# A two-block network on one core: exponentials' clamp and scaling on ScalarE, a later step, and VectorE in program order

## The chip, the cores and the metric

The kernel runs on one core of a Trainium2 chip. The metric is the device time of one execution in microseconds; for the kernel before it is the median of three runs. The engines are TensorE (PE; its weight loads are PEld), VectorE (DVE), ScalarE (ACT), GpSimd (POOL) and SyncE (SP), which issues most of the transfers.

## The reference, cut to what matters

A sequence of 256 tokens of width 1024 goes through a first block of two layers and a second block of two layers. In a layer of the first block, one wide projection feeds a state-space mixer (SSD) and a dilated attention; both are gated, merged, projected, and followed by a gated FFN. In a layer of the second block, one projection feeds a retention and a block-sparse attention; then come an output projection and a gate. The parts that the change touches:

```
# SSD, 32 heads in 4 groups, chunks of 128 tokens
a_cum = cumsum(dt * a)                         # per head, within a chunk
decay = exp(where(causal, a_cum[l] - a_cum[s], -inf))
y_diag = (c @ b.T * decay) @ (x * dt)
decay_states = exp(a_cum[-1] - a_cum)          # first chunk's state for the second
y = group_norm(y * silu(z)) * norm_w           # 4 groups

# dilated attention, 8 heads, three patterns per head
probs_g = exp(scores_g - lse_g);  out = sum_g softmax_g(lse)[g] * probs_g @ v

# entry of the second block
h = rms_norm(x) * norm_final;  u = rms_norm(h) * norm_g
v, q, k = u @ w_in ...
```

## The kernel before, in words

Every weight matrix is read in units of 128 x 1024 values, 488 in all. A unit comes by a transfer (two to a transfer), ScalarE casts it to its high half `wh` (L156), and the rest `wl` is a subtraction (L159), on VectorE, or on GpSimd for every fourth unit while `pool_every` is set, which is from after the dt path to the end of the SSD groups. TensorE then runs each product three times: high by high, high by low, low by high. There are three buffers for halves, and the next unit's halves are made two units ahead (`LEAD = 2`).

The side work (attention, SSD groups, group norms, norms) is written as generators. After each unit of matmuls `tick()` takes one step of each queue in `bg`; `drain` runs queues to their end. The order in which each engine gets its instructions is then set by a scheduler from the program's order and its own model of time, but for regions that `ordered(True, engines)` opens: there the named engines keep the order of the program. Before, only the start of the first block is such a region, and only for SyncE.

Attention (L498) takes four heads of a half, six steps a head: scores with mask and row maximum on VectorE, exponentials with row sums on ScalarE, two sums over the three patterns on GpSimd (L525, L526), a scaling by the reciprocal of the row sum on VectorE (L527, L528), and after two more steps the transposes on TensorE (L387). The first half's attention runs beside the projections of the second half, the second half's beside the B, C and SSD projections; it is drained in the third group at the latest.

An SSD group (L619) fetches the cumulated sums of its 8 heads, copied to all partitions, as `abc` by a transfer on GpSimd's queue (L623). For two heads a step, VectorE takes the minimum of `abc` and the row's own sum (L644), so that the exponent is never above 0; ScalarE makes six exponentials of 128 columns (L653), with the negated sum `nacum` or `rem` as bias; GpSimd multiplies by the masked products `cb` (L654). Two steps later TensorE uses the result (L664). `ssd_tail` (L677) is the group norm: squares, sums, a matmul, a power, a broadcast by matmul, four products (L699) and a split. A group is 12 units long: 4 of x, 4 of z, and 4 of the gate (groups 0 and 1) or of the attention branch (groups 2 and 3).

At the entry of the second block (`block2` with `l == 0`), `proj2` projects v and then q from the normed input before its row factor is known; meanwhile `n1.steps()` finds the factor (L234 to L244), makes the scaled u in four steps of two rows of tiles (L264, L380, L391), and at last scales h (L275).

Of the kernel before, what the change touches and what calls it, by code (L numbers as in the profile page):

```python
# [13 lines left out]
AF = mybir.ActivationFunctionType  # L14
ALU = mybir.AluOpType
# [3 lines left out]
P = 128  # L19
# [265 lines left out]
class Net:  # L285
# [209 lines left out]
            out.append(dst)  # L495
        return out

    def attention(self, v, kT, q0, q1, q2, oh, ol):  # L498
        nc = self.nc
        qs = (q0, q1, q2)  # L500
        scale = HD ** -0.5
        po = None
        for h in range(4):
            e = self.sp.tile([P, 3, 384], F32, tag="EM", name="E", bufs=3)
            m6 = self.small(8, "m6")
            for g in range(3):
                ps = self.ch.tile([P, 384], F32, tag="ch", name="ch")
                nc.tensor.matmul(ps[:, 0:256], qs[g][:, h, 128:256], kT[:, h, :], start=True, stop=True)
                nc.tensor.matmul(ps[:, 256:384], qs[g][:, h, 0:128], kT[:, h, 0:128], start=True, stop=True)
                nc.vector.tensor_tensor_reduce(e[:, g, 0:256], ps[:, 0:256], self.mask_a[:, g, 0:256], 1.0,  # L510
                                               -3e38, ALU.add, ALU.max, m6[:, g:g + 1])
                nc.vector.tensor_tensor_reduce(e[:, g, 256:384], ps[:, 256:384], self.mask_a[:, g, 256:384],
                                               1.0, -3e38, ALU.add, ALU.max, m6[:, 4 + g:5 + g])
            yield
            mx = self.small(4, "mx")
            nc.vector.tensor_reduce(mx[:, 0:2], m6.rearrange("p (i g) -> p i g", i=2)[:, :, 0:3],
                                    mybir.AxisListType.X, ALU.max)
            nc.vector.tensor_scalar(mx[:, 0:2], mx[:, 0:2], -scale, None, op0=ALU.mult)
            nc.scalar.activation(e[:, :, 0:256], e[:, :, 0:256], AF.Exp, bias=mx[:, 0:1], scale=scale,
                                 accum_out=mx[:, 2:3])  # L520
            nc.scalar.activation(e[:, :, 256:384], e[:, :, 256:384], AF.Exp, bias=mx[:, 1:2], scale=scale,
                                 accum_out=mx[:, 3:4])
            yield
            nc.vector.reciprocal(mx[:, 2:4], mx[:, 2:4])
            nc.gpsimd.tensor_tensor(e[:, 0, :], e[:, 0, :], e[:, 1, :], ALU.add)  # L525
            nc.gpsimd.tensor_tensor(e[:, 0, :], e[:, 0, :], e[:, 2, :], ALU.add)  # L526
            nc.vector.tensor_scalar(e[:, 0, 0:256], e[:, 0, 0:256], mx[:, 2:3], None, op0=ALU.mult)  # L527
            nc.vector.tensor_scalar(e[:, 0, 256:384], e[:, 0, 256:384], mx[:, 3:4], None, op0=ALU.mult)  # L528
            yield
            yield  # L530
            pt = self.transpose4([e[:, 0, 256:384], e[:, 0, 0:128], e[:, 0, 128:256]])
            pT = self.sp.tile([P, 384], F32, tag="pT", name="pT", bufs=2)
            nc.scalar.copy(pT, pt[:, 0:384])
            yield
            if h % 2 == 0:
                po = self.ch.tile([P, 2, S], F32, tag="ch", name="ch")
            vs = slice(128 * h, 128 * h + 128)
            nc.tensor.matmul(po[:, h % 2, :], v[:, 0, vs], pT[:, 0:256], start=True, stop=False)
            nc.tensor.matmul(po[:, h % 2, 128:256], v[:, 1, vs], pT[:, 256:384], start=False, stop=True)
            if h % 2:  # L540
                self.split(oh[:, h - 1:h + 1, :], ol[:, h - 1:h + 1, :], po)
            yield

    def dt_path(self, l, xh, xl, wd):

        nc = self.nc
# [13 lines left out]
        def tile2(tag):  # L560
            return self.sp.tile([P, 2, 32], F32, tag=tag, name=tag)

        x, e, z, z2, q = (tile2(n) for n in ("d_x", "d_e", "d_z", "d_z2", "d_q"))
        bias = self.rows[:, 2 * l:2 * l + 1, :].to_broadcast([P, 2, 32])
# [19 lines left out]
        dth = tile2("d_dth")  # L584
# [4 lines left out]
        nc.tensor.matmul(pc[:, 64:96], self.ones, adt[:, 0, :], start=True, stop=True)  # L589
        acum = tile2("d_acum")  # L590
        nc.vector.tensor_copy(acum, pc[:, 0:64].rearrange("p (c h) -> p c h", c=2))
        nacum = tile2("d_nacum")
        nc.vector.tensor_scalar(nacum, acum, -1.0, None, op0=ALU.mult)
        rem = self.small(32, "d_rem", 1)
        nc.vector.tensor_tensor(rem, pc[:, 64:96], acum[:, 0, :], ALU.subtract)
        pr = self.ch.tile([32, S], F32, tag="ch", name="ch")
# [3 lines left out]
        nc.scalar.copy(rows, pr)  # L600
        scr = self.dr.tile([32, S], F32, tag="scr", name="scr")
        nc.gpsimd.dma_start(scr, rows)
        return dth, acum, nacum, rem, scr

    def conv_pair(self, l, ps, ch, dst):

# [11 lines left out]

    def ssd_group(self, l, g, bc, xs, sz, dts, out, tails):  # L619
        nc = self.nc  # L620
        dth, acum, nacum, rem, scr = dts
        abc = self.sp.tile([P, 8, S], F32, tag="abc", name="abc")
        nc.gpsimd.dma_start(abc, scr[8 * g:8 * g + 8, :].partition_broadcast(P))  # L623
        pc = self.ch.tile([P, 384], F32, tag="ch", name="ch")
# [13 lines left out]
        for step in range(6):  # L638
            if step < 4:
                m = ms[step] = self.sp.tile([P, 2, 384], F32, tag="EM", name="M", bufs=3)  # L640
                h0 = 8 * g + 2 * step

                mb = m.rearrange("p j (b c) -> p j b c", b=3)
                nc.vector.tensor_tensor(  # L644
                    mb[:, :, 0:3:2, :], abc[:, 2 * step:2 * step + 2, :].rearrange("p j (b c) -> p j b c", b=2),
                    acum[:, :, h0:h0 + 2].rearrange("p b j -> p j b")[:, :, :, None].to_broadcast([P, 2, 2, P]),
                    ALU.min)
                for j in range(2):
                    hh = h0 + j
                    for b, src, bias in ((0, m[:, j, 0:128], nacum[:, 0, hh:hh + 1]),  # L650
                                         (1, abc[:, 2 * step + j, 128:256], rem[:, hh:hh + 1]),
                                         (2, m[:, j, 256:384], nacum[:, 1, hh:hh + 1])):
                        nc.scalar.activation(m[:, j, 128 * b:128 * b + 128], src, AF.Exp, bias=bias)  # L653
                nc.gpsimd.tensor_tensor(m, m, cb[:, None, :].to_broadcast([P, 2, 384]), ALU.mult)  # L654
            if step >= 2:
                pr = step - 2
                m = ms.pop(pr)
                if pr % 2 == 0:
                    yps = self.ch.tile([P, 2, S], F32, tag="ch", name="ch")

                for c, qs, ks in ((0, slice(0, 256), slice(0, 256)), (1, slice(128, 256), slice(256, 384))):
                    for j in range(2):
                        h = 2 * pr + j
                        nc.tensor.matmul(yps[64 * j:64 * j + 64, pr % 2, qs], xdt[:, c, 64 * h:64 * h + 64],  # L664
                                         m[:, j, ks], start=c == 0, stop=c == 1)
                if pr % 2:
                    for j in range(2):
                        f = pr - 1 + j
                        nc.vector.scalar_tensor_tensor(xs[:, f, :], xs[:, f, :], dsk[:, 4 * g + f:4 * g + f + 1],
                                                       yps[:, j, :], ALU.mult, ALU.add)  # L670
                    nc.gpsimd.tensor_tensor(xs[:, pr - 1:pr + 1, :], xs[:, pr - 1:pr + 1, :],
                                            sz[:, pr - 1:pr + 1, :], ALU.mult)
            if step == 5:
                tails.append(self.ssd_tail(l, g, xs, out))
            yield

    def ssd_tail(self, l, g, xs, out):  # L677
        nc = self.nc
# [1 line left out]
        nc.scalar.activation(sq, xs, AF.Square)  # L680
        nc.gpsimd.tensor_tensor(sq[:, 0:2, :], sq[:, 0:2, :], sq[:, 2:4, :], ALU.add)
        nc.gpsimd.tensor_tensor(sq[:, 0, :], sq[:, 0, :], sq[:, 1, :], ALU.add)
        for _ in range(4 if g == 3 else 6):
            yield
        pss = self.ch.tile([P, 2], F32, tag="ch", name="ch")
        for t in range(2):
# [16 lines left out]
    def block1(self, l, h, n1):  # L703
        nc = self.nc
        a = self.a
        qn, qa, qs, qt = [n1.steps()], [], [], []
# [19 lines left out]
        os = [self.pair([P, 4, S], "O0", "O1")]  # L726
# [9 lines left out]
        for f in range(0, 8, 2):  # L736
            ps = self.pairA("w_in", l, C_B + 128 * f, D, getu)
            self.conv_pair(l, ps, 16 + f, bc[:, f:f + 2, :])
            if f == 0:
                self.drain(qa)  # L740
                os.append(self.pair([P, 4, S], "A0", "A1"))
                qa.append(self.attention(*B, *os[1]))
        def halves(tiles):
            return [tiles[f // 4][:, f % 4:f % 4 + 2, :] for f in range(0, 8, 2)]

# [317 lines left out]
    def block2(self, l, x, n1):  # L1063
# [7 lines left out]
        def tile(tag, shape, bufs=1):  # L1071
            return sp.tile([P, *shape], F32, tag=tag, name="b2", bufs=bufs)

        qn, qm, qr = [n1.steps()], [], []
        self.bg = [qn, qm, qr]
        mv = tile("B2", [2, 512])
        self.proj2(l, 6, n1.get, "v", mv, norm=n1)
        if l == 0:
# [1 line left out]
        mq = tile("B0", [4, S])  # L1080
        self.proj2(l, 4, n1.get, "q", mq, qm, hg[:, 0, :], norm=n1)
        self.drain(qn)
        getu = n1.getv
        mk = tile("B1", [4, S])
        self.proj2(l, 5, getu, "k", mk, qm, hg[:, 1, :])
# [166 lines left out]
```

## Time and profile before

| | |
|---|---|
| median of 3 runs | 1570.98 us (1570.22 to 1572.79) |
| profiled execution | 1576.56 us, span 1574.8 us |
| PE busy | 1541.3 us |
| DVE busy | 1163.3 us |
| ACT busy | 826.6 us |
| POOL busy | 462.5 us |
| mean granted clock of TensorE | 0.993 |

The span is from the first instruction to the last. A busy time is the share of the span in which the engine had an instruction running; an engine that is idle and not on the path costs nothing. The granted clock is the share of TensorE's full clock; 1.00 is the full level and 0.50 the lower one.

### The profile page before, as it was taken

The numbers are of one execution on the slowest core, as the hardware profiler recorded it, in microseconds if no ns is written. First come the engines' busy times: TensorE is split into PE (matmuls) and PEld (weight loads), VectorE is DVE, ScalarE is ACT, GpSimd is POOL, SyncE is SP. The second block draws the span as 40 slices with busy tenths as digits, with TensorE's granted clock in tenths as the row PEclk, the third lists the DMA queues.
The fourth block names the chain that finished last, engine by engine and source line by source line (L and its number), as shares of the span: only waits on it lengthen the run. The fifth ranks groups of instructions, "written<-read, shape, count | busy, mean of one in ns | idle before, by whom it ended". The sixth has DMA issues, their size and how long they took to land.

```text
span 1574.8 us, 29400 instructions
## 1 busy us (share of the span) xinstructions
PE 1541.3 (98%) x12104; PEld 1478.2 (94%) x12104; DVE 1163.3 (74%) x1758; ACT 826.6 (52%) x1276; POOL 462.5 (29%) x285
## 2 busy tenths in 40 slices
PE   9999999989999999999999999999999999999998
PEld 7999999889999999999998999998999979998998
DVE  7888998765577565668897887567655578788776
ACT  6444567545455444544466765445444454456443
POOL 4656356543000000066525565110000112111110
PEclk9999999989999999999999999999999999999999
DMA  8644544445554555554443455455555545455542
GB/s 307 234 167 139 184 162 161 149 146 191 188 182 166 188 187 188 191 210 161 157 166 135 182 193 199 169 203 207 181 184 182 184 159 185 136 188 187 188 147 95
DMA packets 42662, 280.68 MB, mean 178 GB/s; under 512 B 4864, under 2 KB 7040, under 8 KB 10016
## 3 DMA queue, kind: packets, MB, share of 16 engines
q1 hardware_dynamic: 40592, 267.20, 47.9%
q0 software_dynamic: 1936, 11.60, 1.9%
q8 instruction: 95, 1.56, 0.4%
q14 instruction: 39, 0.32, 0.1%
HBM read 274.53 MB, written 4.26 MB: 177 GB/s over the span
## 4 chain that ended last, share of the span: by engine, by line
PE 85%; DVE 8%; ACT 2%; issue 2%; POOL 2%; DMA 1%; DVEq 0%; SPq 0%; POOLq 0%; ACTq 0%
PE mm L451 17%; PE mm L453 17%; PE mm L452 17%; PE mm L435 6%; PE mm L436 6%; PE mm L437 6%; PE mm L399 3%; PE mm L398 3%; PE mm L400 3%; DVE wl L159 2%; PE ch L664 1%; PE tr L387 1%; ACT wh L156 1%; DVE acc L614 1%; DVE E L527 1%
## 5 line engine op out<-in xcount | busy, mean ns | idle before, releaser
L156 ACT CAST wh<-raw 128x1024 fp32r<-128x1024 f32 x488 | 511.0, 1048 | 570.3 <-PE mm L452 381.6
L159 DVE TENSOR_TENSOR wl<-raw,wh 128x1024 fp32r<-128x1024 f32 x456 | 606.1, 1332 | 259.2 <-ACT wh L156 255.7
L453 PE MATMUL mm<-uh,wl 128*128 128x256 f32 x2240 | 629.3, 281 | 5.8 <-DVE wl L159 3.7
L451 PE MATMUL mm<-uh,wh 128*128 128x256 f32 x2240 | 633.2, 283 | 0.1
L452 PE MATMUL mm<-ul,wh 128*128 128x256 f32 x2240 | 627.5, 280 | 0.0
L453 PEld LDWEIGHTS mm<-uh,wl 128*128 128x128 f32 x2240 | 422.9, 189 | 7.3 <-DVE wl L159 4.6
L451 PEld LDWEIGHTS mm<-uh,wh 128*128 128x128 f32 x2240 | 422.6, 189 | 5.1 <-issue 3.5
L452 PEld LDWEIGHTS mm<-ul,wh 128*128 128x128 f32 x2240 | 425.0, 190 | 0.7 <-issue 0.3
L208 POOL TENSOR_TENSOR nsq<-nsq 128x512 f32<-128x512 f32 x19 | 29.7, 1570 | 484.6 <-ACT nsq L202 405.7
L159 POOL TENSOR_TENSOR wl<-raw,wh 128x1024 fp32r<-128x1024 f32 x32 | 79.0, 2470 | 68.2 <-ACT wh L156 63.1
L435 PE MATMUL mm<-A,wh 128*128 128x256 f32 x288 | 82.1, 285 | 1.0 <-ACT wh L156 1.0
L437 PE MATMUL mm<-A,wl 128*128 128x256 f32 x288 | 81.6, 285 | 0.1
L399 PE MATMUL mm<-wl,nu 128*128 128x512 f32 x192 | 77.1, 403 | 2.9 <-DVE wl L159 2.8
L654 POOL TENSOR_TENSOR M<-M,cb 128x768 f32<-128x768 f32 x32 | 69.8, 2197 | 25.7 <-ACT M L653 17.7
L400 PE MATMUL mm<-wh,nu 128*128 128x512 f32 x192 | 76.0, 399 | 0.0
L398 PE MATMUL mm<-wh,nu 128*128 128x512 f32 x192 | 72.6, 401 | 3.0 <-DVE tg L827 2.2
L614 DVE SCALAR_TENSOR_TENSOR acc<-mm,feat,acc 128x255 f32<-128x255 f32 (+1 forms) x144 | 67.2, 475 | 5.1 <-ACT acc L612 3.7
L471 POOL TENSOR_TENSOR qT<-qT,rot 64x512 f32<-64x512 f32 x32 | 56.7, 1773 | 48.5 <-ACT qT L467 48.5
L472 POOL TENSOR_TENSOR qT<-qT,rp 64x512 f32<-64x512 f32 x32 | 60.1, 1877 | 28.3 <-DVE rp L469 28.1
L436 PE MATMUL mm<-A,wh 128*128 128x256 f32 x224 | 63.8, 285 | 0.0
L435 PEld LDWEIGHTS mm<-A,wh 128*128 128x128 f32 x288 | 55.0, 191 | 1.4 <-ACT wh L156 1.3
L437 PEld LDWEIGHTS mm<-A,wl 128*128 128x128 f32 x288 | 54.8, 191 | 0.6 <-DVE wl L159 0.6
(311 smaller groups left out, 2984.3 us busy)
## 6 DMA issues: line engine op xcount, KB each, us to landing
raw<-in_w_dram SPq DMA_DIRECT2D x243, 1024.0 KB, 4.8
abc<-scr POOLq DMA_DIRECT2D x8, 1024.0 KB, 5.3
es<-e POOLq DMA_DIRECT2D x4, 512.0 KB, 4.3
e<-es SPq DMA_DIRECT2D x4, 512.0 KB, 4.5
raw<-in_w_dram SPq DMA_DIRECT2D x2, 512.0 KB, 4.4
h<-in_xT_dram SPq DMA_DIRECT2D x2, 512.0 KB, 9.4
h<-in_xT_dram SPq DMA_DIRECT2D x1, 1024.0 KB, 4.9
hs<-h POOLq DMA_DIRECT2D x1, 1024.0 KB, 5.9
```

What stands on the lines that cost most here:

```text
L156: self.nc.scalar.copy(h, raw)
L159: eng.tensor_tensor(lo, raw, h.bitcast(F32), ALU.subtract)
L398: nc.tensor.matmul(ps, xh[:, k0 + k, ts], hw[:, k, :], start=start and k == 0, stop=False)
L399: nc.tensor.matmul(ps, xh[:, k0 + k, ts], lw[:, k, :], start=False, stop=False)
L400: nc.tensor.matmul(ps, xl[:, k0 + k, ts], hw[:, k, :], start=False, stop=stop and k == 1)
L435: nc.tensor.matmul(ps, hw[:, n % 8, :], xh[:, kx, :], start=opens, stop=False)
L436: nc.tensor.matmul(ps, hw[:, n % 8, :], xl[:, kx, :], start=False, stop=False)
L437: nc.tensor.matmul(ps, lw[:, n % 8, :], xh[:, kx, :], start=False, stop=left[f] == 0)
L451: nc.tensor.matmul(ps, hw[:, k, :], xh[:, kx, :], start=j == 0 and k == 0, stop=False)
L452: nc.tensor.matmul(ps, hw[:, k, :], xl[:, kx, :], start=False, stop=False)
L453: nc.tensor.matmul(ps, lw[:, k, :], xh[:, kx, :], start=False, stop=j == n - 1 and k == 7)
L614: nc.vector.scalar_tensor_tensor(acc[:, j, k:S], ps[:, j, 0:S - k], w[:, 3 - k:4 - k], acc[:, j, k:S], ALU.mult, ALU.add)
```

## The change

Five edits. The clamp of the SSD exponents moves from a VectorE minimum to ScalarE: four Relu of 128 columns (of the row's sum minus `abc`), and one exponential over all four results with scale -1; the two `rem` exponentials stay. `nacum` is no longer made. The scaling of E in attention moves from VectorE to ScalarE. The second half's attention takes one step more in each head before its transposes. The group norms of groups 0 to 2 take one step more before their matmul. And in `block2` of its first layer VectorE keeps program order from the v projection to the end of `n1`'s steps.

```
-    def attention(self, v, kT, q0, q1, q2, oh, ol):
+    def attention(self, v, kT, q0, q1, q2, oh, ol, late=0):
...
-            nc.vector.tensor_scalar(e[:, 0, 0:256], e[:, 0, 0:256], mx[:, 2:3], None, op0=ALU.mult)
-            nc.vector.tensor_scalar(e[:, 0, 256:384], e[:, 0, 256:384], mx[:, 3:4], None, op0=ALU.mult)
-            yield
-            yield
+            nc.scalar.activation(e[:, 0, 0:256], e[:, 0, 0:256], AF.Identity, scale=mx[:, 2:3])
+            nc.scalar.activation(e[:, 0, 256:384], e[:, 0, 256:384], AF.Identity, scale=mx[:, 3:4])
+            yield
+            yield
+            for _ in range(late):
+                yield
...
-        nacum = tile2("d_nacum")
-        nc.vector.tensor_scalar(nacum, acum, -1.0, None, op0=ALU.mult)
...
-                nc.vector.tensor_tensor(
-                    mb[:, :, 0:3:2, :], abc[:, 2 * step:2 * step + 2, :].rearrange("p j (b c) -> p j b c", b=2),
-                    acum[:, :, h0:h0 + 2].rearrange("p b j -> p j b")[:, :, :, None].to_broadcast([P, 2, 2, P]),
-                    ALU.min)
                 for j in range(2):
                     hh = h0 + j
-                    for b, src, bias in ((0, m[:, j, 0:128], nacum[:, 0, hh:hh + 1]),
-                                         (1, abc[:, 2 * step + j, 128:256], rem[:, hh:hh + 1]),
-                                         (2, m[:, j, 256:384], nacum[:, 1, hh:hh + 1])):
-                        nc.scalar.activation(m[:, j, 128 * b:128 * b + 128], src, AF.Exp, bias=bias)
+                    a2 = abc[:, 2 * step + j, :]
+                    for c in range(2):
+                        nc.scalar.activation(mb[:, j, 2 * c, :], a2[:, 128 * c:128 * c + 128], AF.Relu, scale=-1.0,
+                                             bias=acum[:, c, hh:hh + 1])
+                    nc.scalar.activation(mb[:, j, 1, :], a2[:, 128:256], AF.Exp, bias=rem[:, hh:hh + 1])
+                nc.scalar.activation(mb[:, :, 0:3:2, :], mb[:, :, 0:3:2, :], AF.Exp, scale=-1.0)
...
-        for _ in range(4 if g == 3 else 6):
+        for _ in range(4 if g == 3 else 7):
             yield
...
-                qa.append(self.attention(*B, *os[1]))
+                qa.append(self.attention(*B, *os[1], 1))
...
+        if l == 0:
+            self.ordered(True, {mybir.EngineType.DVE})
         mv = tile("B2", [2, 512])
         self.proj2(l, 6, n1.get, "v", mv, norm=n1)
...
         self.drain(qn)
+        self.ordered(False)
```

## Rows read from the trace of the kernel before

**Rows 1.** Page, part 1: busy us, share of the span, instructions.
```profile
PE 1541.3 (98%) x12104; PEld 1478.2 (94%) x12104; DVE 1163.3 (74%) x1758; ACT 826.6 (52%) x1276; POOL 462.5 (29%) x285
```

**Rows 2.** Waits of TensorE, 90 to 260: us in total, times, longest.
```profile
PE tr L387 <- DVE E L528: 2.4, 3, 1.2
PE mm L453 <- DVE wl L159: 1.1, 1, 1.1
```

**Rows 3.** Waits of TensorE, 270 to 360.
```profile
PE mm L453 <- DVE wl L159: 4.8, 2, 2.4
PE mm L453 <- POOL wl L159: 1.9, 1, 1.9
PE tr L387 <- DVE xs L617: 1.5, 2, 0.7
```

**Rows 4.** Waits of TensorE, 720 to 860.
```profile
PE mm L453 <- DVE wl L159: 2.5, 2, 1.3
PE tr L387 <- DVE E L528: 2.2, 2, 1.9
...
PE tr L387 <- DVE mx L518: 0.7, 1, 0.7
```

**Rows 5.** Waits of TensorE, 1250 to 1300.
```profile
PE mm L399 <- DVE wl L159: 2.1, 1, 2.1
```

**Rows 6.** Windows: busy PE, PEld, DVE, ACT, POOL; then clock, DMA share, GB/s.
```profile
275.00:375.00 100.00, 91.65 (x721) 86.49 (x718) 67.80 (x89) 51.22 (x88) 51.46 (x27) 0.93 0.44 160
825.00:850.00 25.00, 22.41 (x168) 20.67 (x167) 21.67 (x42) 17.70 (x43) 13.23 (x8) 0.93 0.36 122
1275.00:1300.00 25.00, 22.93 (x103) 18.17 (x102) 19.82 (x41) 14.21 (x44) 3.02 (x3) 0.93 0.42 139
200.00:250.00 50.00, 48.68 (x402) 46.07 (x401) 45.46 (x83) 37.62 (x82) 30.49 (x19) 1.00 0.42 149
```

**Rows 7.** Groups on ScalarE: shapes, count, busy us, mean ns, idle before.
```profile
L653 ACT ACTIVATE M<-M,d_nacum 128x128 f32<-128x128 f32 x128 | 40.5, 389 | 8.4 <-DVE M L644 8.4
...
L202 ACT ACTIVATE nsq<-h 128x512 f32<-128x512 f32 x32 | 20.0, 625 | 1.3 <-DVE h L857 1.2 <-POOL nsq L208 0.2
...
L380 ACT ACT_TABLE_LOAD x1 | 1.3, 1283 | 0.7 <-PEq L1241 0.7
```

**Rows 8.** Groups on VectorE, the same columns.
```profile
L644 DVE TENSOR_TENSOR M<-abc,d_acum 128x512 f32<-128x512 f32 x32 | 29.6, 936 | 17.2 <-DMA abc<-scr 13.3 <-PE ch L664 3.2 <-PE tr L387 0.7
...
L527 DVE TENSOR_SCALAR E<-E,mx 128x256 f32<-128x256 f32 x16 | 21.1, 1321 | 12.0 <-POOL E L526 11.9
...
L528 DVE TENSOR_SCALAR E<-E,mx 128x128 f32<-128x128 f32 x16 | 9.8, 610 | 0.0
```

**Rows 9.** Timeline of VectorE and of GpSimd near 185: start, us, instruction.
```profile
185.67 2.45 DVE L527 TENSOR_SCALAR E<-E,mx 128x256 f32<-128x256 f32 x1 [0.51 <-POOL E L526]
...
185.60 2.37 POOL L159 TENSOR_TENSOR wl<-raw,wh 128x1024 fp32r<-128x1024 f32 x1
```

**Rows 10.** Timeline of ScalarE, 311 to 331.
```profile
321.11 0.40 ACT L653 ACTIVATE M<-abc,d_rem 128x128 f32<-128x128 f32 x1 [7.63 <-DMA abc<-scr]
...
325.59 1.03 ACT L156 CAST wh<-raw 128x1024 fp32r<-128x1024 f32 x1
```

**Rows 11.** Timeline of VectorE and of ScalarE (two casts), 1263 to 1291.
```profile
1270.16 0.16 DVE L244 TENSOR_TENSOR nr<-nr,nr 128x2 f32<-128x2 f32 x1 [0.81 <-POOL nr L373]
...
1273.51 3.22 DVE L264 SCALAR_TENSOR_TENSOR nv<-h,g,ch 128x256 f32<-128x256 f32 x8 [0.94 <-PE ch L225]
...
1277.82 0.69 DVE L391 TENSOR_TENSOR ul<-nv,uh 128x512 fp32r<-128x512 f32 x1
...
1280.98 1.22 DVE L159 TENSOR_TENSOR wl<-raw,wh 128x1024 fp32r<-128x1024 f32 x1
...
1266.59 1.05 ACT L156 CAST wh<-raw 128x1024 fp32r<-128x1024 f32 x1 [1.68 <-PE mm L400]
...
1274.41 0.62 ACT L380 CAST uh<-nv 128x512 fp32r<-128x512 f32 x1 [1.94 <-DVE nv L264]
```

More of the change, by code (lines that the diff above doesn't have):

```diff
@@ L602, in dt_path @@
         nc.gpsimd.dma_start(scr, rows)
-        return dth, acum, nacum, rem, scr
+        return dth, acum, rem, scr
     def conv_pair(self, l, ps, ch, dst):
@@ L620, in ssd_group @@
         nc = self.nc
-        dth, acum, nacum, rem, scr = dts
+        dth, acum, rem, scr = dts
         abc = self.sp.tile([P, 8, S], F32, tag="abc", name="abc")
```

## The prediction

> **What bounds the kernel.** I read the page first. TensorE is busy 1541.3 of 1574.8 us [rows 1], so what any change of the side work can give back is the other 33.5 us, plus what the clock costs. Next came the waits of TensorE by stage, then the granted clock by windows, then the shapes on ScalarE and VectorE that the diff touches, and last the order on the engines at four places.
>
> The reader is to see four groups of stalls. The first lies where attention runs beside projections. In layer 0, transposes of E wait 2.4 us for VectorE's scaling of E, and one matmul waits 1.1 us for a low half [rows 2]; in layer 1 the same two kinds cost 2.2 and 2.5 us, and a transpose loses 0.7 us to a tiny VectorE instruction [rows 4]. That is 8.9 us in all. The second lies in the later SSD groups of layer 0: 4.8, 1.9 and 1.5 us, together 8.2 us [rows 3]. The third is the entry of block 2: 2.1 us [rows 5].
>
> The fourth is the clock. It is at its full level (2.4 GHz) nearly everywhere, but it fell to the lower one (1.2 GHz) for a while after the long idle spells: it is 0.93 over 275 to 375, over 825 to 850 and over 1275 to 1300 [rows 6]. The time lost is (1 - 0.93) times the length: 7.0, 1.8 and 1.8 us. So a stall near 2 us or longer costs up to twice itself here.
>
> All this is latency, not throughput. Each unit needs a cast on ScalarE, then a subtraction on VectorE (in places on GpSimd), two units ahead. Anything that stands in front of either in its queue eats that lead. Around the attention VectorE is the fuller of the two: 45.5 of 50 us in 200 to 250, against 37.6 on ScalarE [rows 6].
>
> **Clamp.** VectorE loses 32 instructions of 0.94 us, 29.6 us busy, and 17.2 us of idle time ahead of them, mostly waits for the abc transfer [rows 8]. With them goes the small negation (nacum), which I cost at nothing: one instruction of 64 columns a layer, so at most two of the 0.61 us that one of 128 columns takes [rows 8], behind cumulated sums that no stall in the four groups waits for. ScalarE gets 128 Relu of 128 columns and 32 exponentials of 512 columns for 128 exponentials of 128 columns. By busy time the old ones took 40.5/128 = 0.32 us each; I price a Relu the same, since it has the same shape and the same kind of bias operand. The wide exponential I price as the Square of that width, 20.0/32 = 0.63 us [rows 7]. So the Relu replace the exponentials at no cost, and ScalarE gains 32 x 0.63 = 20 us. Two things the trace does not show. One is a ScalarE instruction that reads what ScalarE has just written, as the wide exponential does; I bound that by nothing below and by one more short instruction, 0.39 us, above, 12 us in all on ScalarE, and take nothing because the last of four Relu is all it can wait for. The other is Relu itself: the run holds one table load, 1.28 us [rows 7], for all the functions used; if Relu needed its own, two loads a step would be 64 x 1.28 = 82 us. I take nothing, as the nearest rows are the many functions that share the one load. The Trainium skill, "ScalarE: Activation LUTs" (Table sets), says that relu is in every set; no run shown has a Relu.
>
> **Does it pay?** The chain of a step was one VectorE instruction of 0.94 us and six short ones; now it is six short ones and a wide one. It ends about 0.3 us earlier (0.94 against 0.63), but ScalarE is held 0.63 us longer. GpSimd's masking behind it starts no later. Alongside, VectorE no longer queues low halves behind a clamp that waits for abc; ScalarE did wait there and still does, 7.63 us once [rows 10].
>
> The Trainium skill, the same page (Rules for kernel authors), speaks against the edit: relu, max and min belong on VectorE, not ScalarE. By it the clamp costs 4 x 0.32 = 1.27 us on ScalarE for 0.94 us on VectorE, 32 x 0.33 = 10.6 us more in engine time, which would be lost in full if engine time set the end. The rows agree on the price, but engine time does not set the end here; the queue does, which is the rival below.
>
> **Scaling of E.** VectorE loses 16 x (1.32 + 0.61), 30.9 us, and the 12.0 us ahead of it in which it waited for GpSimd's sum [rows 8]. ScalarE gains 16 x (0.47 + 0.32) = 12.6 us; 0.47, for 256 columns, lies halfway between the 0.32 of 128 columns and the 0.63 of 512, which are the bounds [rows 7]. The long VectorE times are not work: at 185.67 the scaling took 2.45 us beside a GpSimd subtraction from 185.60 that took 2.37 us [rows 9]; GpSimd's instructions hold it up. ScalarE would have finished the same pair by about 186.5 instead of after 188.1, more than the 1.2 us that TensorE waited there. But the 12.0 us wait for GpSimd moves to ScalarE with it, and the casts are behind it.
>
> **One step more for heads.** It moves the transposes of the second attention one unit back, with the copy, two matmuls and split behind them. It issues nothing new and no transfer. Four heads take 28 steps instead of 24; the drain comes 38 steps after the start (6 of B and C, two groups of 12, 8 of the third group), so nothing is late. At the worst place (1.9 us, part of the 2.2) the transpose goes behind other matmuls.
>
> **One step more for group norms.** Groups 0 to 2 take 10 steps of tail instead of 9, in a period of 12, so a tail still ends before the next begins; no transfer is moved. The two small sums, the power on GpSimd, the broadcast, four VectorE products and the split come one unit later. That takes four products and a low half out of the crowded stretch ahead of the branch units where 4.8 us are lost. Not out of the queue before the late instruction, though, so I give it little.
>
> **The order of VectorE in block 2.** Before, eight products (3.22 us from 1273.51) and the products of L275 are ahead of the low half at 1280.98 that TensorE waits for [rows 11]. In program order, low halves alternate with two products and one low part of u. I worked it through: the first low half in question comes behind the norm's chain, which ends at 1270.32, so at 1271.6, where it is wanted soon after 1270. (A cast of 1.05 us at 1266.59 came after 1.68 us of waiting for TensorE to free its buffer, so a unit takes about 2.8 us with the hand-over; one unit and the norm's small matmuls lie between that release and this low half.) After that each unit costs VectorE 1.2 for the low half, 0.8 for two products, 0.6 of waiting for ScalarE's cast and 0.7 for the low part [rows 11], some 3.3 to 3.4 us with the hand-overs, against a unit of 2.8 us. So TensorE would stall four times for about 0.6 us and once for 0.5 to 1.4, 3 to 4 us, where now it loses 2.1 + 1.8 = 3.9. The short stalls may spare the clock. Bounds: all 3.9 back, or 2 us lost if the clock falls too. I take 1 us gained.
>
> **The sum.** Attention: 8.9 us of stalls and 1.8 us of clock, 10.7; three quarters go, 8.0 us. The quarter left is for transposes that then wait for ScalarE and for low halves that GpSimd's own subtractions hold up, which nothing here moves. SSD groups: 8.2 + 7.0 = 15.2 us; GpSimd's load there stays, VectorE loses only the clamps; one quarter, 3.8 us. Block 2: 1 us. Against it, new waits for casts behind 33 us more on ScalarE: nothing to 20 us by the rival below, taken as 3 us, about two stalls like those of 1.1 us with some clock. Together 8.0 + 3.8 + 1 - 3 = 9.8 us. The profiled execution took 1576.56 us, 1.8 more than its span and 5.6 more than the median 1570.98; taken from the median, 1570.98 - 9.8 = 1561.2 us.
>
> **Rivals.** *All stalls go* (0.20): freeing VectorE also frees GpSimd, and the later tail opens the crowded stretch. 10.7 + 15.2 + 3.9 - 3 = 26.8 us, 1544.2 us. For it: 60 us leave the engine that is late in most rows. Against: the 1.9 us are a GpSimd low half behind a late cast [rows 3].
>
> *The gain is hidden* (0.17): the stalls of the SSD groups stay, and ScalarE's waits take the place of VectorE's. 3 us or less, 1568 to 1574. For it: the sum of E by GpSimd comes no sooner.
>
> *ScalarE's queue becomes the bound, slower* (0.18). Place: after abc lands, at 321.11, ScalarE runs three steps of clamps and exponentials and only at 325.59 the cast [rows 10] that the 1.9 us wait hangs on [rows 3]. Two steps stand ahead of that cast, and at 0.63 us each it comes 1.3 us later; with as much again in clock, 2.6 us a group. In all eight groups that is 20.8 us; after the gains of the attention and block 2 (9 us), 1583 us. It decides from five groups on (13 us). The Trainium skill's rule on relu, named above, would come true this way. A table load for every Relu is in its tail.
>
> **How the numbers follow.** My forecast, part of the stalls gone, has 0.45 and its own range 1555 to 1567. With the first rival, faster has 0.65; same 0.17; slower 0.18. 0.2% is 3.1 us, about what a measurement of this kernel can tell from no change. The range 1549 to 1577 leaves out the better part of the full gain and the worse part of the slower case, about 0.2.
>
> **What would show it.** Right: no transpose waits for E; ScalarE near 860 us, VectorE near 1100; the low halves after the heads earlier; no clock drop near 845. Wrong: TensorE waiting for casts, or for low halves whose cast was behind a Relu; new clock drops in the groups; five stalls of 1 us or more near 1275; more than one table load. The prediction fails most likely in the groups, where I guess a quarter of 15.2 us.

## The result and the profile after

The changed kernel takes 1560.73 us (median of 4 runs, 1560.51 to 1563.3) beside 1570.6 us for the kernel before on the same chip: ratio 0.9941, interval 0.9928 to 0.9954, so faster by 0.6%. The forecast was 1561.2. Its profiled execution took 1563.3 us with a span of 1561.2; against the span before this is 13.6 us less, more than the 9.9 us by which the medians differ, because the profiled execution before lay 6.0 us above its median and the one after only 2.6.

Part 1 of the page after, beside [rows 1]:

```profile
PE 1535.5 (98%) x12104; PEld 1472.7 (94%) x12104; DVE 1112.6 (71%) x1692; ACT 854.9 (55%) x1340; POOL 472.2 (30%) x285
```

Waits of TensorE after, in four stretches. From 90 to 260 it has none at all, where [rows 2] has 3.5 us. Here are 270 to 360, 720 to 960 and 1250 to 1300, beside [rows 3 to 5]:

```profile
PE mm L453 <- POOL wl L159: 3.1, 2, 1.6
PE mm L451 <- DVE acc L614: 0.8, 2, 0.5
...
PE mm L451 <- DVE sz L765: 2.7, 1, 2.7
PE ch L685 <- POOL sq L680: 2.3, 1, 2.3
PE mm L453 <- POOL wl L159: 1.0, 1, 1.0
...
PE mm L399 <- DVE wl L159: 2.6, 5, 1.1
```

The windows of [rows 6] after, and one more at the place of the new waits:

```profile
275.00:375.00 100.00, 96.08 (x808) 90.72 (x807) 66.96 (x86) 59.19 (x98) 59.06 (x30) 1.00 0.48 170
825.00:850.00 25.00, 25.00 (x213) 23.22 (x207) 15.65 (x32) 18.71 (x43) 16.25 (x11) 1.00 0.47 169
1275.00:1300.00 25.00, 23.95 (x172) 22.07 (x171) 22.59 (x44) 10.59 (x24) 4.29 (x4) 1.00 0.43 153
200.00:250.00 50.00, 50.00 (x417) 47.68 (x416) 35.64 (x67) 41.55 (x88) 31.48 (x19) 1.00 0.44 158
...
885.00:910.00 25.00, 20.05 (x150) 19.62 (x150) 16.14 (x21) 12.90 (x20) 14.66 (x8) 0.86 0.30 98
```

The reader is to see that three of the four groups of stalls shrank or went, and that a new one came. Attention: 8.9 us of waits and 1.8 of clock are gone. Groups of layer 0: 8.2 us of waits are 3.9 now, and 7.0 us of clock are back. Block 2: 2.1 and 1.8 us are 2.6 of short waits at the full clock. New: in a group of layer 1 TensorE waits 2.3 us for a sum of the group norm's squares on GpSimd, 2.7 us for the product that finishes silu(z) on VectorE (L765; z's product from here on), and, one group earlier, 1.0 us for a low half; the clock behind them costs (1 - 0.86) x 25 = 3.5 us. The sum is 10.7 + 11.3 + 1.3 - 9.5 = 13.8 us, near the 13.6 of the spans. It is not exact: where the clock fell before a wait was over, the two are counted twice. By TensorE's totals 5.8 us of the 13.6 are busy time (1541.3 to 1535.5) and 7.8 us are idle time.

What the moved work costs on ScalarE after (beside [rows 7]):

```profile
L648 ACT ACTIVATE M<-abc,d_acum 128x128 f32<-128x128 f32 x128 | 44.0, 392 | 9.6 <-DMA abc<-scr 5.4 <-PE ch L662 4.0
L651 ACT ACTIVATE M<-M 128x512 f32<-128x512 f32 x32 | 19.8, 622 | 0.0
L527 ACT ACTIVATE E<-E,mx 128x256 f32<-128x256 f32 x16 | 8.1, 506 | 8.7 <-POOL E L526 8.7
L528 ACT ACTIVATE E<-E,mx 128x128 f32<-128x128 f32 x16 | 6.2, 388 | 0.0
L380 ACT ACT_TABLE_LOAD x1 | 1.3, 1283 | 0.7 <-PEq L1242 0.7
```

And the new stall in the timeline, 884 to 900, first VectorE, then GpSimd (start, us, instruction):

```profile
891.68 2.51 DVE L159 TENSOR_TENSOR wl<-raw,wh 128x1024 fp32r<-128x1024 f32 x1
...
894.89 2.73 DVE L159 TENSOR_TENSOR wl<-raw,wh 128x1024 fp32r<-128x1024 f32 x1
897.55 0.15 DVE L372 TENSOR_SCALAR rs_v<-ch 128x2 f32<-128x2 f32 x1
897.62 0.67 DVE L765 SCALAR_TENSOR_TENSOR sz<-sz,mm 128x512 f32<-128x512 f32 x1
```

```profile
887.22 1.30 POOL L679 TENSOR_TENSOR sq<-sq 128x512 f32<-128x512 f32 x1 [4.35 <-ACT sq L678]
888.47 4.63 POOL L652 TENSOR_TENSOR M<-M,cb 128x768 f32<-128x768 f32 x2
893.07 1.70 POOL L680 TENSOR_TENSOR sq<-sq 128x256 f32<-128x256 f32 x1
```

Between the two halves of the group norm's sum (L679, L680) GpSimd runs two masking products of the next group, 4.63 us. TensorE's matmul over the sum comes at 894.83, when L680 is done. Then the low halves on VectorE, 2.51 and 2.73 us where 1.22 is usual [rows 11], hold up z's product, which frees TensorE's next accumulator. That GpSimd makes them long can be read from the trace before: of 456 low halves on VectorE, 301 ran with no GpSimd instruction beside them, and none of these took more than 1.23 us. The order of GpSimd's queue alone does not make the stall: in layer 0 two products stand between the halves of the sum in two groups of the changed kernel as well, and no matmul of L685 waits there.

### The profile page after: what moved, and what is told of

It reads as the page before. It is cut to its first block, busy times and chain, and to the rows that moved or that the text cites. A ratio compares the mean times of both kernels' runs of the same rounds, so it can differ in the third digit from the quotient of the medians.

```text
span 1561.2 us, 29384 instructions
## 1 busy us (share of the span) xinstructions
PE 1535.5 (98%) x12104; PEld 1472.7 (94%) x12104; DVE 1112.6 (71%) x1692; ACT 854.9 (55%) x1340; POOL 472.2 (30%) x285
## 5 line engine op out<-in xcount | busy, mean ns | idle before, releaser
L614 DVE SCALAR_TENSOR_TENSOR acc<-mm,feat,acc 128x255 f32<-128x255 f32 (+2 forms) x144 | 67.4, 477 | 12.6 <-ACT acc L612 10.9
```

## The experiments

All ratios are to the kernel before on the same chip.

| run | what it is | median us | ratio [interval] |
|---|---|---|---|
| s_scale | before, scaling of E on ScalarE | 1559.83 | 0.9934 [0.9912, 0.9956] |
| s_clamp | before, clamp on ScalarE | 1568.06 | 0.9985 [0.9968, 1.0001] |
| s_order | before, VectorE's order in block 2 | 1570.34 | 1.0005 [0.9992, 1.0019] |
| s_steps | before, both later steps | 1576.76 | 1.0028 [1.0004, 1.0053] |
| a_noclamp | after, clamp back on VectorE | 1551.05 | 0.9874 [0.9851, 0.9897] |
| a_nosteps | after, both steps back | 1562.09 | 0.9950 [0.9933, 0.9968] |
| a_notail | after, group norm's step back | 1559.62 | 0.9909 [0.9881, 0.9937] |
| a_notlate | after, heads' step back | 1570.73 | 0.9993 [0.9975, 1.0011] |
| a_double | after, 20 us more on ScalarE | 1559.50 | 0.9929 [0.9901, 0.9956] |
| a_nopool | after, no low halves on GpSimd | 1586.32 | 1.0098 [1.0063, 1.0134] |
| a_vsum1 | after, L680 on VectorE | 1569.59 | 0.9980 [0.9961, 0.9998] |
| n_vsum1 | a_noclamp, its L680 on VectorE | 1554.94 | 0.9878 [0.9835, 0.9922] |

### Each part alone

**s_scale.** The kernel before with

```
-            nc.vector.tensor_scalar(e[:, 0, 0:256], e[:, 0, 0:256], mx[:, 2:3], None, op0=ALU.mult)
+            nc.scalar.activation(e[:, 0, 0:256], e[:, 0, 0:256], AF.Identity, scale=mx[:, 2:3])
```

and the same for the 128 columns.

> The kernel before with only the scaling of E moved to ScalarE. Theory of the prediction (VectorE's queue is relieved): the 2.4 and 2.2 us that transposes wait for the scaling of E go, and the low halves late after a head (1.1 us at 110, 1.2 us at 732) with them, so at least 6 us of the 10.7 us of the attention stalls and their clock; 1562 to 1566 us, the group stalls (4.8, 1.9, 1.5 us) still there. Rival (the step moved the transposes and that is what counted): transposes wait for ScalarE's scaling instead, 4 to 5 us; 1569 to 1572 us.

Measured: 1559.83 us, below the theory's range and as much as the whole change gives. TensorE has no wait from 90 to 260, so all of [rows 2] is gone. From 720 to 860 all of [rows 4] is gone too, but one wait of 2.3 us is new (a group's product, L664, for VectorE's mask and maximum, L512). The groups of layer 0 are as they were, clock and all, as a row of its waits from 200 to 360 and then its window 275 to 375 show beside [rows 3, 6]:

```profile
PE mm L453 <- DVE wl L159: 5.0, 3, 2.4
```

```profile
275.00:375.00 100.00, 91.41 (x718) 86.33 (x717) 67.78 (x86) 48.49 (x77) 49.05 (x27) 0.93 0.46 160
```

So moving the scaling is enough for the attention's gain, and it gives nothing in the groups of layer 0.

**s_clamp.** The kernel before with the clamp's lines of the change (L648 to L651 and no `nacum`).

> The kernel before with only the clamp moved to ScalarE (four Relu and one wide exponential a step, no negated sums). Theory: the attention stalls stay (about 9 us), the SSD groups lose a part of their 15.2 us, some 4 to 11 us; 1560 to 1567 us. Rival (ScalarE's queue becomes the bound): casts come 1.3 us later behind each batch of clamps and TensorE waits for them; 1572 to 1583 us.

Measured: 0.9985, with an interval that touches 1; 1568.06 us lies just above the theory's range and below the rival's. The groups of layer 0 wait 3.6 us instead of 8.2 from 270 to 360 and keep their clock, 1.00 over 275 to 375 for 0.93, so the clamp's move alone does what the whole change does there. The attention's waits for E and for VectorE's low halves do not stay as expected either: 4.2 us are left of the 8.2 in [rows 2, 4]. But other waits come, of 1.7 us each at a group's products (L662) and at the group norm's sum (L685), and the clock falls behind both.

**s_order.** The kernel before with VectorE's program order from the v projection to the end of `n1`'s steps.

> The kernel before with only the program order for VectorE at the entry of block 2. Theory: one stall of 2.1 us and the clock drop near 1283 (1.8 us) give way to about five stalls of 0.3 to 1 us; 1 to 2 us gained, 1569 to 1570 us, all else as before. Rival (the order does all it says): 3.9 us gained, 1567 us. Rival (the order blocks VectorE behind the norm's chain): 1572 us or more.

Measured: no difference. Its waits from 1250 to 1300 read as after (2.6 us in five, longest 1.1) at a granted clock of 1.00, so by the profile 3.9 us became 2.6. A gain of 1.3 us lies at the edge of the interval (0.9992) and can't be told from nothing.

**s_steps.** The kernel before with the heads' and the group norms' step.

> The kernel before with only the two later steps (heads of the second attention, group norms of groups 0 to 2). Theory: the transposes of the second attention no longer wait (1.2 us in layer 0, 1.9 to 2.6 us and a clock drop of 1.8 us in layer 1), the groups stay as they are; 1564 to 1568 us. Rival (any change of the program sets another order on all engines, and the gain is luck): stalls at new places, 1566 to 1576 us.

Measured: slower, 1.0028, with an interval that starts at 1.0004. The stalls are at new places, as the rival says. The waits for E in the whole run, and the timeline at the longest of them, 222 to 235, on VectorE and then on GpSimd:

```profile
PE tr L387 <- DVE E L528: 8.9, 5, 4.8
```

```profile
226.20 1.19 DVE L527 TENSOR_SCALAR E<-E,mx 128x256 f32<-128x256 f32 x1
227.31 5.90 DVE L528 TENSOR_SCALAR E<-E,mx 128x128 f32<-128x128 f32 x1
```

```profile
227.78 1.29 POOL L673 TENSOR_TENSOR xs<-xs,sz 128x512 f32<-128x512 f32 x1
229.03 1.80 POOL L656 TENSOR_TENSOR M<-M,cb 128x768 f32<-128x768 f32 x1
230.79 2.33 POOL L159 TENSOR_TENSOR wl<-raw,wh 128x1024 fp32r<-128x1024 f32 x1
```

The scaling of 128 columns took 5.90 us and ended at 233.21, when GpSimd's third instruction in a row ended (233.12). Before, it took 0.61 us in the mean [rows 8]: 0.27 or 0.28 in the 11 of 16 with no GpSimd instruction beside them, 0.82 to 1.85 in the others. In this version's order it stands beside a group's masking; which of the two steps put it there was not run. One group of layer 0 also has three masking products between the halves of its sum, and TensorE waits 2.6 us for an accumulation near them. The Trainium skill, "SBUF — State Buffer" (Who interferes with whom), says that VectorE in its two-port modes contends with GpSimd, and with two inputs from SBUF with GpSimd instructions that read SBUF, and that whoever issues first holds the ports for the whole instruction. The row, a scaling with one input, agrees in kind if it ran in a two-port mode, which no run here shows, and goes further: the wait lasted over three instructions of GpSimd.

### Parts taken back

**a_noclamp.** After, with the minimum on VectorE and `nacum` as before.

> The changed kernel with the clamp back on VectorE (scaling of E on ScalarE, both later steps, the order in block 2 stay). Theory (the scaling of E is what pays, the clamp is worth little on top of it): 1558 to 1564 us, no attention stalls, the group stalls of layer 0 back at about 8 us and their clock drops, none of the 2.3 and 2.7 us in the groups of layer 1. Rival (the clamp pays 4 us or more on top): 1565 us or more.

Measured: 1551.05 us, which beats both kernels, lies below the theory's range and rules out the rival. Its window at the place of the new stall, and GpSimd's timeline there:

```profile
885.00:910.00 25.00, 25.00 (x213) 24.50 (x212) 19.09 (x28) 13.42 (x19) 15.85 (x8) 1.00 0.48 169
```

```profile
885.05 1.30 POOL L683 TENSOR_TENSOR sq<-sq 128x512 f32<-128x512 f32 x1 [1.89 <-ACT sq L682]
886.43 1.60 POOL L684 TENSOR_TENSOR sq<-sq 128x256 f32<-128x256 f32 x1
```

The two halves of the sum are adjacent here, and TensorE is busy 25.00 of 25 us at the full clock. Against 20.05 at 0.86 in the changed kernel that is 4.95 + 3.5 = 8.5 us, while the spans (1554.0 and 1561.2) differ by 7.2. In layer 0 a_noclamp is the worse of the two: it waits 3.3 us for an accumulation (L616), and its clock is 0.97 over 275 to 375.

So between these two profiles the difference lies at this place. It is not shown to be the whole cost of the clamp. In a_notail and a_double, described below, the clamp is on ScalarE too, no masking product stands between the halves of the sum, and the window at this place, in this order, is nearly full:

```profile
885.00:910.00 25.00, 24.34 (x205) 23.47 (x204) 23.70 (x30) 15.64 (x25) 16.07 (x8) 1.00 0.49 169
```

```profile
885.00:910.00 25.00, 23.47 (x196) 22.92 (x195) 18.95 (x24) 16.97 (x28) 17.31 (x9) 1.00 0.42 147
```

Yet they take 1559.62 and 1559.50 us (ratios 0.9909 and 0.9929, against 0.9874). Each differs from a_noclamp in one part more, but with the stall gone half or more of the clamp's cost is still there.

**a_nosteps.** After, without both steps.

> The changed kernel without the two later steps. Theory (the steps only shift which instructions meet on GpSimd): 1557 to 1564 us; the 2.3 us wait of the group norm's matmul for GpSimd's sum stays or grows to 3 us, since that matmul comes one unit earlier; no transposes wait for E even without the step for heads. Rival (the steps are needed once ScalarE scales E): transposes wait for ScalarE, 1 to 2 us in each layer, 1564 to 1570 us.

Measured: 0.9950 beside 0.9941. Without the steps TensorE's transposes wait for the convolved `xs` (L617), 5.4 us in three, and for L680 2.3 us. On top of the clamp the two steps together give nothing that can be told.

**a_notail** and **a_notlate.** After, with one step back each:

```
-        for _ in range(4 if g == 3 else 7):
+        for _ in range(4 if g == 3 else 6):
```

```
-                qa.append(self.attention(*B, *os[1], 1))
+                qa.append(self.attention(*B, *os[1]))
```

> The changed kernel with the group norm's step taken back (6 instead of 7), the heads' step kept. Theory of the order: GpSimd then runs both sums before the masking products of the next group, no L685 waits for more than 1 us, and the stall of 2.7 us behind it goes too: 1553 us (1550 to 1557). Rival, the group norm's step is what helps in the other groups (it kept the four products out of the branch units): stalls of tr L387 and mm L453 of 2 us each come back in groups 1 and 2, 1562 us or more.

> The changed kernel with the heads' step taken back, the group norm's step kept. If the heads' step has no part in the result, as the prediction took it: 1559 to 1563 us, the same stalls at L685. If it is what the scaling needed (a transpose that now waits for ScalarE): transposes wait for E again, 1 to 2 us in two to four places, 1564 to 1570 us.

Waits of TensorE from 720 to 960, first a_notail, then a_notlate:

```profile
PE mm L451 <- DVE sz L765: 2.3, 1, 2.3
PE ch L685 <- POOL sq L680: 1.9, 2, 1.3
```

```profile
PE mm L451 <- DVE sz L765: 5.3, 2, 2.7
PE ch L685 <- POOL sq L680: 4.5, 2, 2.4
PE tr L387 <- DVE xs L617: 1.7, 2, 1.5
```

a_notail: 1559.62 us, not the 1553 of the theory and not the rival's either. Its L680 is ahead of the masking again, the longest wait of L685 falls to 1.3 us and the clock holds, but z's product is still late. The order costs 5 us by the ratios (0.9909 against 0.9941, on intervals that just overlap), about 1 us by the medians. a_notlate: 1570.73 us, and by another way than either theory: no transpose waits for E. The pair of stalls at L685 and at z's product now comes in two groups of layer 1. So the heads' step, which the prediction took for harmless, is worth 8 us by the ratios (0.9993 against 0.9941). The trace shows masking between the halves of the sum in one group more without it (four for three); how one step of the heads decides that, the runs don't show.

The traces of all versions with the sum on GpSimd show what this order goes with. Without the group norm's later step (before, s_scale, s_clamp, s_order, a_nosteps, a_notail) no masking product stands between the halves in any group. With it there are three products in one group of s_steps and of a_noclamp, and two products in three groups of the changed kernel and in four of a_notlate and of a_nopool; only a_double has the step and none. So the step opens the way for this order, and the clamp on ScalarE mostly makes it more frequent.

### What is the limit: engine time or order

**a_double.** After, with a second pass over each wide result:

```
+                nc.scalar.activation(mb[:, :, 0:3:2, :], mb[:, :, 0:3:2, :], AF.Identity)
```

> The changed kernel with a second pass of ScalarE over each step's wide exponential (an identity in place, the values stay), 32 x 0.63 = 20 us more on ScalarE and each step that much longer. Theory (ScalarE has room): 0 to 4 us, 1560 to 1565 us. Rival (ScalarE's queue is the next bound): 10 to 20 us, 1571 to 1581 us, TensorE waiting for casts or for low halves whose cast came late in the groups.

Measured: 1559.50 us with 20 us more on ScalarE, the same time. From 90 to 1400 us no matmul waits for a cast. The order on the other engines changed as well: the stall at L685 and L765 in layer 1 is gone, and waits of 2.3 us (a low half) and 1.9 us (an accumulation) come in layer 0, so the equal time is a balance. The low half was not behind a late cast: its cast had ended by 289.35, and VectorE took 2.98 us for it, from 290.70, beside GpSimd. The load on ScalarE is not the bound, and casts behind it are not what the clamp costs.

**a_nopool.** After, with `POOL_EVERY = 0`: all low halves on VectorE.

> The changed kernel with every low half on VectorE (POOL_EVERY = 0, so 32 subtractions of 2.5 us leave GpSimd and 32 of about 1.3 us go to VectorE). Theory (what is left in the groups is GpSimd's queue and VectorE held up beside it): the stalls of the groups in both layers, 8.8 us and 3.4 us of clock, fall to 4 us or less; 1550 to 1557 us. Rival (VectorE has no room for them): low halves late in the groups and beside the second attention, 1562 to 1572 us.

Measured: slower by 1%, outside both ranges. GpSimd lost 80 us of work, and masking products then stood between the halves of the sum in four groups. Waits of TensorE in the whole run:

```profile
PE ch L685 <- POOL sq L680: 12.7, 4, 3.3
PE mm L451 <- DVE sz L765: 10.8, 4, 3.0
```

**a_vsum1** and **n_vsum1.** After, and a_noclamp, with the second half of the sum on VectorE:

```
-        nc.gpsimd.tensor_tensor(sq[:, 0, :], sq[:, 0, :], sq[:, 1, :], ALU.add)
+        nc.vector.tensor_tensor(sq[:, 0, :], sq[:, 0, :], sq[:, 1, :], ALU.add)
```

> The changed kernel with the second sum of the group norm's squares (128x256) on VectorE instead of GpSimd; all else as changed. Theory of the order on GpSimd: with the clamp on ScalarE and the later group norm, this sum stands behind two masking products in groups 1 and 2 of both layers, and TensorE waits for it (2.3 us at 894.8), then for the gate product (2.7 us) and loses 3.4 us of clock. With the sum on VectorE no matmul of L685 waits for GpSimd, and about 8 us come back: 1553 us (1550 to 1556). Rival, ScalarE's 20 us of added work delay the casts wherever they fall: the sum makes no difference, 1558 to 1564 us.

> The changed kernel with the clamp back on VectorE (which ran in 1551.05 us) and the second sum of squares on VectorE as well. Theory of the order: there the sum was behind the masking products in one group only (group 2 of layer 0), where TensorE lost 3.3 us and 3.4 us of clock; if that is the cause, 1545 us (1543 to 1548). Rival, that stall is an accumulation on VectorE with a cause of its own: 1549 to 1553 us.

a_vsum1 took 1569.59 us; both theories missed. No matmul of L685 waits any more, but another wait takes its place. A row of its waits, and the timeline from 278 to 292 of VectorE and then of GpSimd:

```profile
PE mm L451 <- DVE acc L614: 9.6, 2, 4.8
```

```profile
280.23 2.08 DVE L680 TENSOR_TENSOR sq<-sq 128x256 f32<-128x256 f32 x1
282.23 0.47 DVE L614 SCALAR_TENSOR_TENSOR acc<-mm,feat,acc 128x255 f32<-128x255 f32 x1
282.62 2.46 DVE L159 TENSOR_TENSOR wl<-raw,wh 128x1024 fp32r<-128x1024 f32 x1
285.01 0.86 DVE L614 SCALAR_TENSOR_TENSOR acc<-mm,feat,acc 128x254 f32<-128x254 f32 x2
285.80 2.04 DVE L159 TENSOR_TENSOR wl<-raw,wh 128x1024 fp32r<-128x1024 f32 x1
```

```profile
279.18 7.57 POOL L652 TENSOR_TENSOR M<-M,cb 128x768 f32<-128x768 f32 x3
```

Three masking products follow each other for 7.57 us, and beside them VectorE's sum takes 2.08 us and its low halves 2.46 and 2.04. The convolution's accumulations stand between them in the queue, come late, and TensorE's next unit has no free accumulator. So the late sum is not the whole matter: VectorE's instructions are held up while the masking runs, whichever engine has the sum. n_vsum1 shows the same at a_noclamp's one stall: 1554.94 us, a little above its rival's range and by the ratios the same as a_noclamp, and the wait grew from 3.3 us:

```profile
PE mm L451 <- DVE rs_v L372: 5.3, 1, 5.3
```

## Why the prediction was right, point by point

The time was right to 0.5 us, but some terms were not, and they cancelled; so much nearness is luck. The terms below come from the two profiles, which differ by 13.6 us, the medians by 9.9, and the forecast took its 9.8 from the median.

**Attention: right, by its own mechanism.** 8.0 us were taken of 10.7; all 10.7 went, and s_scale shows that moving the scaling is enough for it. The quarter kept for transposes that wait for ScalarE was not there. ScalarE's scaling costs 0.51 and 0.39 us, where the prediction took 0.47 and 0.32; VectorE's went up to 5.90 beside GpSimd (s_steps).

**SSD groups: too small in layer 0, and layer 1 not foreseen.** A quarter of 15.2 us was taken, 3.8; 11.3 came back in layer 0, and s_clamp has nearly the same (waits of 3.6 us at the full clock), so there the clamp's move is enough, as the prediction reasoned. Layer 1's groups, which had no stall before, lost 9.5 us. The net, 1.8 us, is near the 3.8 only because a larger gain and a loss that no term held stand against each other.

**The 3 us of new waits: the size too small, the kind wrong.** They were to be casts behind ScalarE's added work. No such wait shows, and a_double adds 20 us to ScalarE at no cost. The new waits are for GpSimd's sum and for z's product on VectorE. With this the rival of ScalarE's queue falls. The prices held: a Relu costs 0.34 us (44.0/128) for the 0.32 predicted, the wide exponential 0.62 for 0.63, and there is one table load. The Trainium skill's advice to keep relu, min and mul on VectorE ("ScalarE: Activation LUTs", Rules for kernel authors) came out right for the clamp on top of the rest, by some 10 us, though not through engine time, and wrong for the scaling, which is a mul. For the instruction by itself it holds there too: 256 columns took VectorE 0.34 us with no GpSimd instruction beside it, and ScalarE 0.51; it is GpSimd that turns it round.

**The clamp: "Does it pay?" failed.** Alone it may gain 2.4 us; on top of the rest it costs 0.0067 of the time, some 10 us (0.9941 against 0.9874). The prediction looked at the chain of one step and at what VectorE no longer queues. It held that GpSimd's masking "starts no later" and did not ask where the scheduler would then put the products: in the changed kernel they come between the two halves of the group norm's sum and lengthen VectorE's low halves beside them. How much of the 10 us that is stays open, since a_notail and a_double lack that order and still come to 1559.6 and 1559.5. Of what the prediction named as proof, no transpose waiting for E, the busy times near 860 and 1100, and no fall of the clock near 845 came true. Of what it named as signs of being wrong, one came true as well: a new fall of the clock in a group, at 897.

**The later steps: the step that failed most.** "Nothing is late" and "I give it little". Alone they are slightly slower, in the trace through a scaling beside the masking and through new stalls in the groups. With the clamp on VectorE, scaling, both steps and block 2's order together stand at 0.9874, scaling alone at 0.9934: 9 us for the rest by the difference of two runs, of which block 2 has 1.3 at most. With the clamp on ScalarE, from 0.9950 without either, the heads' step alone goes to 0.9909 (6 us gained), the norms' step alone to 0.9993 (7 us lost), both to 0.9941 (1 us gained). The prediction expected the norms' step to thin out a crowded stretch; the traces show that it lets masking products in between the halves of the sum.

**Block 2: right.** 1 us was taken, 1.3 us by the profile; five waits and no fall of the clock, 2.6 us in all for the 3 to 4 worked out. In the time it can't be told.

What stays open: why a_notail and a_double, which have no masking product between the halves of the sum, do not come to 1551 us. In layer 1 of a_notail z's product is still late once (2.3 us) and the sum twice (1.3 us at most). a_noclamp without the norms' step was not run, so the best set of parts isn't known. A version that keeps VectorE's instructions off the masking products altogether was not tried. The best version run is the change without the clamp.

## What to carry to other kernels

A change of several small parts under a scheduler is not the sum of its parts: here the scaling alone gave as much as the whole, the steps were a small loss alone and by difference most of 9 us of gain on top of it, and the clamp gave nothing clear of noise alone (2.4 us by the medians) and cost 10 us on top. Take each part out of the finished change as well as adding it alone, and look at what stands between two instructions of a short chain on each in-order queue. Where VectorE and GpSimd run side by side, read the duration of the same instruction at both places before moving work between engines.

## What the runs showed of the hardware

A VectorE scaling of 128 columns took 0.27 or 0.28 us with no GpSimd instruction beside it, and 5.90 us beside three of them in a row; on ScalarE it took 0.39 us in the mean. A low half on VectorE took 1.22 us in the mean and 1.23 at most with no GpSimd instruction beside it, and 2.0 to 2.7 in the rows beside masking that are shown here. Taking 80 us of work from GpSimd made the kernel 1% slower, and adding 20 us to ScalarE left the time as it was. The clock fell behind the stalls of 2.3 and 2.7 us in the changed kernel, and held through one of 2.3 us in a_notail, so not every such stall costs it.
